# Attention trunk on one core: the V projection with the weights held still and a DMA transpose, one output store per pair and group, small operations in pairs

## The chip, the cores and the metric

The kernel runs on 1 core of one Trainium2 chip. The metric is the device time of one execution, in microseconds (us). Engines are named as in the profile: PE (TensorE matmul), PEld (its weight load), DVE (VectorE), ACT (ScalarE), POOL (GpSimd), SP (SyncE, here only a DMA queue).

## The reference, cut to what matters

One layer on x of 2048 tokens by 1024. The input projection gives q, k and v of 8 heads of banded attention (kind A) and of 4 pairs of heads of differential attention (kind B). What the change touches is the projection, both attentions and the way of their output into the output projection:

```python
h = rmsnorm(x, attn_norm_g[l])
proj = h @ w_in[l]
qa, ka, va, qb, kb, vb = jnp.split(proj, 6, axis=-1)
...
# kind A: 64-wide heads, 9 chunks of 64 keys behind and at the query's chunk
scores = jnp.where(valid, scores + bias[:, None], -jnp.inf)
p = jax.nn.softmax(scores, axis=-1).astype(v.dtype)
o = jnp.einsum("bhcqk,bckhd->bcqhd", p, vb)
...
# kind B: all earlier chunks, two maps per head
p = jax.nn.softmax(sc, axis=-1).reshape(b, B_HEADS, 2, Q_BLOCK, s)
w = p[:, :, 0] - lam * p[:, :, 1]
o = jnp.einsum("bhqk,bkhe->bqhe", w.astype(v.dtype), v)
...
x = x + jnp.concatenate([oa, ob], axis=-1) @ w_out[l]
```

Behind it stand a gated feed-forward part with a causal convolution and a last rmsnorm, which the change leaves alone.

## The kernel before

**Numbers.** Every matrix product is made of float16 halves: a value is split into a high and a low half (`split`: ACT writes the high one, DVE or POOL the low one), and a product is three matmuls per block of 128 rows (`TERMS`: high by high, high by low, low by high). With eight blocks of 128 in D a projection is 24 matmuls.

**Stages.** The attention part works pair of heads by pair of heads, in the order `ORDER = [4, 5, 0, 6, 1, 7, 2, 3]`: numbers from 4 up are kind B (`attn_b`), the others kind A (`attn_a`). A pair holds 128 columns of each of Q, K and V. Within a pair there are four groups of 512 tokens (`tg`), and in a group four tiles of 128 queries. The stages lie from about 100 to 1300 us: B 100 to 280, B 280 to 450, A 450 to 565, B 565 to 745, A 745 to 860, B 860 to 1040, then two A. After them come the output projection, whose first half fills the last stage, and the feed-forward part.

**One tile.** `scores` (L417, L419) makes 128 queries by up to 512 keys; DVE adds the bias and takes the running maximum (L466 in A, L516 in B); `nb` (L472, L520) turns the maximum into the exponent's bias, one operation per head; ACT takes the exponential (L473, L522) with its row sum. In B a tile wider than 1024 keys has two halves, whose row sums are added per head (L525); then the two maps are combined with `ratio` (L538 on DVE; for the second half of odd tiles L535 on ACT and L536 on POOL). The result is split into `phl` (ACT L474 or L540; low half on POOL L475 or L541, in A for one head on DVE), transposed by a DMA on SP into `pt` (L476, L543), multiplied with V (L487, L549) and scaled into `osb` (L489, L551).

**A group's end.** `store_oT` splits `osb` into `ohl` (L427 ACT, L428 DVE), transposes it on SP into `ost` (L432), and stores it with four DMAs on POOL (L437) into `oTd[NT, P, 2, NC-1, P]` in DRAM. The last pair's `ost_l` stays in SBUF. `out_proj` loads one tile of `oTd` at a time (L606), 3584 bytes per partition in one piece.

**Projections.** `project` (L365 to L374) holds the weights of Q or K still and streams 512 tokens: 24 matmuls 128x512. `proj_v` (L385 to L398) does it the other way round, since V is wanted with tokens on partitions: a tile of h is held still, the weights of 128 columns are streamed, 4 x 24 matmuls 128x128, and the sum is split straight into `vs`.

**What sets the order.** In the main loop a pair's stage first prepares the next pair's weights (`load_w`: DMA, squares on DVE, the scaling L331 and low half L333 on POOL, the high half L332 on ACT). Then for each group it writes Q of the next group, the group's four tiles at a raised priority, and K and V of the next pair for the same group. A scheduler makes each engine's order from priorities and its own times, so that the projections of the next pair fill PE between the tiles. Score rows are kept in "granules", one pool of 8 buffers: a B tile over 1024 keys takes four, the others two. There are four weight buffers `whl`, which the loads `oT` use later, and two `wraw`.

## Time and profile before

| What | Value |
|---|---|
| runs | 2644.75, 2649.1, 2653.84 us; median 2649.1 |
| the profiled execution | 2652.78 us, of it span 2651.0 us, mean granted clock of TensorE 0.95 |
| PE busy | 2405.8 us (91%) |
| DVE busy | 1949.0 us (74%) |
| ACT busy | 1402.0 us (53%) |
| POOL busy | 1246.5 us (47%) |

The shares are means over the attention, the output projection and the feed-forward part. The change touches the first two only, so the argument goes by stretches of time: the busy time of each engine in a stretch, and the rows of single instructions with their start and length. The granted clock is 1.00 at 2.4 GHz and 0.50 at 1.2 GHz; a mean between them is a mixture.

### The profile page before, as it was taken

To read this page: it belongs to the slowest core of one execution; us is meant where nothing else is said; L and a number is where in the kernel's file an instruction comes from. 1 tells how busy PE (TensorE), PEld (TensorE's weight loads), DVE (VectorE), ACT (ScalarE), POOL (GpSimd) and SP (SyncE) were. 2 spreads that over 40 slices of the span, in tenths; PEclk is the share of its full clock that TensorE was granted. 3 is DMA by queue.
4 is the path that set the end of the run, shared out by engine and by line. 5 is a ranking of instruction groups with operands and counts; after the bars stand their busy time and mean duration, and the time that the engine had idled before them with its cause. 6 is when DMAs were issued, how large, how long until landed. Compare 5 with 4: busy or idle time off the path is not lost.

```text
span 2651.0 us, 43815 instructions
## 1 busy us (share of the span) xinstructions
PE 2405.8 (91%) x15894; PEld 1245.1 (47%) x15894; DVE 1949.0 (74%) x4551; ACT 1402.0 (53%) x2431; POOL 1246.5 (47%) x1239
## 2 busy tenths in 40 slices
PE   5798897979788896899986999999999999999998
PEld 4554454545455454554432444444444444444443
DVE  6778798658976687676675688888887887656655
ACT  5456466545655466565543556666656564333332
POOL 2324345342542335222243466655566655756654
PEclk8899898989899897999988999999999999999999
DMA  7233445643465336778979533333333338432322
GB/s 205 55 60 75 85 83 109 113 99 60 85 120 111 73 68 151 147 175 199 282 231 218 139 105 124 109 100 124 111 113 121 100 102 320 174 107 86 126 91 76
DMA packets 571016, 333.42 MB, mean 126 GB/s; under 512 B 392024, under 2 KB 533648, under 8 KB 569392
## 3 DMA queue, kind: packets, MB, share of 16 engines
q1 hardware_dynamic: 551456, 301.46, 44.0%
q0 software_dynamic: 6752, 18.91, 2.4%
q10 hardware_dynamic: 12592, 10.26, 1.4%
q8 instruction: 124, 2.03, 0.3%
q14 instruction: 92, 0.75, 0.1%
HBM read 148.87 MB, written 85.21 MB: 88 GB/s over the span
## 4 chain that ended last, share of the span: by engine, by line
PE 37%; DVE 4%; POOL 3%; DMA 3%; issue 3%; ACT 2%; SPq 0%; DVEq 0%; ACTq 0%; POOLq 0%
PE mm L752 22%; PE mm L1151 13%; PE omm L616 2%; DMA wd<-gd 1%; DMA wdraw<-in_w_down_dram 1%; POOL wuhl L870 1%; ACT wuraw L852 1%; DVE Y L951 1%; DVE wdhl L782 1%; DVE hl L640 1%; DMA td<-hl 0%; ACT wdhl L779 0%; POOL wd L1128 0%; ACT Y L955 0%; SPq L986 0%
## 5 line engine op out<-in xcount | busy, mean ns | idle before, releaser
L752 PE MATMUL mm<-T,wuhl 128*128 128x512 f16 x3696 | 807.2, 381 | 28.1 <-ACT tmp L923 24.5
L752 PEld LDWEIGHTS <-wuhl 128*128 128x128 f16 x3696 | 362.7, 99 | 464.8 <-issue 34.5
L1151 PE MATMUL mm<-wd,ghl 128*128 128x512 f16 x1848 | 401.8, 380 | 3.4 <-ACT ghl L127 2.1
L372 PE MATMUL mm<-h,whl 128*128 128x512 f16 x1536 | 370.5, 390 | 0.0
L541 POOL TENSOR_TENSOR phl<-St,phl 128x1024 f16<-128x1024 f32 (+4 forms) x96 | 162.3, 1725 | 291.5 <-ACT phl L540 276.8
L417 PE MATMUL s<-ks,qs 128*128 128x128 f16 (+3 forms) x720 | 198.5, 298 | 101.5 <-DVE mx L466 47.2
L1151 PEld LDWEIGHTS <-ghl 128*128 128x128 f16 x1848 | 180.7, 98 | 223.8 <-ACT ghl L127 3.6
L951 DVE SCALAR_TENSOR_TENSOR Y<-U,taps,Y 128x1024 f32<-128x1024 f32 x176 | 256.6, 1458 | 4.0 <-ACT Y L947 2.4
L393 PE MATMUL mm<-whl,h 128*128 128x128 f16 x3072 | 236.6, 226 | 2.9 <-ACT h L127 2.9
L522 ACT ACTIVATE St<-St,nb,sc 128x1024 f32<-128x1024 f32 (+4 forms) x192 | 188.4, 982 | 85.1 <-DVE nb L520 80.9
L372 PEld LDWEIGHTS <-whl 128*128 128x128 f16 x1536 | 146.1, 101 | 173.8 <-issue 26.4
L127 ACT ACTIVATE ghl<-wd,gsc 128x384 f16<-128x384 f32 (+1 forms) x176 | 106.4, 659 | 197.1 <-DMA wd<-gd 90.2
L393 PEld LDWEIGHTS <-h 128*128 128x128 f16 x3072 | 186.8, 101 | 48.6 <-issue 24.4
L128 DVE SCALAR_TENSOR_TENSOR ghl<-wd,gsc,ghl 128x384 f16<-128x384 f32 (+1 forms) x176 | 137.5, 816 | 94.4 <-ACT ghl L127 93.7
L419 PE MATMUL s<-ks,qs 64*128 64x128 f16 (+3 forms) x720 | 187.3, 303 | 0.9 <-DVE qs L128 0.9
L475 POOL TENSOR_TENSOR phl<-St,phl 128x640 f16<-128x640 f32 (+2 forms) x64 | 84.4, 1339 | 219.6 <-ACT phl L474 195.9
L516 DVE CUSTOM_DVE_ANT_0 St<-s,near,mxb 128x512 f32<-128x512 f32 (+3 forms) x280 | 170.1, 624 | 23.5 <-PE s L419 18.9
L616 PE MATMUL omm<-wohl,oT 128*128 128x512 f16 x672 | 157.4, 387 | 13.9 <-DVE x L620 13.9
L861 POOL TENSOR_TENSOR Sx<-wuraw 128x512 f32<-128x512 f32 x44 | 78.0, 1775 | 168.8 <-ACT wuraw L852 159.8
L419 PEld LDWEIGHTS <-qs 64*128 64x128 f16 x720 | 57.6, 93 | 206.8 <-issue 186.1
L473 ACT ACTIVATE St<-St,nb,sc 128x640 f32<-128x640 f32 (+4 forms) x128 | 108.1, 845 | 77.0 <-DVE nb L472 76.0
L955 ACT ACTIVATE Y<-Y 128x1024 f32<-128x1024 f32 x44 | 46.5, 1057 | 183.8 <-DVE Y L951 183.8
(226 smaller groups left out, 4217.1 us busy)
## 6 DMA issues: line engine op xcount, KB each, us to landing
wd<-gd SPq DMA_DIRECT2D x88, 256.0 KB, 2.8
wuraw<-in_w_up_dram SPq DMA_DIRECT2D x42, 512.0 KB, 5.1
gd<-Y SPq DMA_DIRECT2D x42, 512.0 KB, 4.9
wdraw<-in_w_down_dram SPq DMA_DIRECT2D x154, 128.0 KB, 2.7
wd<-wdd SPq DMA_DIRECT2D x11, 1792.0 KB, 12.4
wdd<-wdhl SPq DMA_DIRECT2D x41, 448.0 KB, 2.6
wraw<-in_w_in_dram SPq DMA_DIRECT2D x24, 512.0 KB, 4.5
td<-hl SPq DMA_DIRECT2D x24, 512.0 KB, 3.9
```

The source lines that it names most:

```text
L128: V.scalar_tensor_tensor(lo, src, scale, hi, ALU.mult, ALU.subtract)
L372: nc.tensor.matmul(ps, lhsT=hl[:, a, c, :], rhs=h[:, b, c, :], start=n == 0, stop=n == 3 * NC - 1)
L393: nc.tensor.matmul(ps[:, t], lhsT=h[:, a, c, t * P:(t + 1) * P], rhs=hl[:, b, c, :], start=n == 0, stop=n == 3 * NC - 1)
L417: nc.tensor.matmul(ps[hd], lhsT=qs[:, hd, 0, qc], rhs=ks[:, hd, kc], start=True, stop=False)
L419: nc.tensor.matmul(ps[hd], lhsT=qs[a:b, hd, 1, qc], rhs=ks[a:b, hd, kc], start=False, stop=True)
L516: V.tensor_tensor_reduce(Sm[hd][g][:, a0:a0 + b - a], ps[hd][:, :b - a], bias, 1.0, m[hd], ALU.add, ALU.max, mx[:, hd, f:f + 1])
L522: A.activation(Sm[hd][g], Sm[hd][g], AF.Exp, bias=nb[:, hd:hd + 1], scale=w["sc"], accum_out=l[:, hd, g:g + 1])
L541: nc.gpsimd.tensor_tensor(hl[:, 1], Sm[0][g], hl[:, 0], ALU.subtract)
L616: nc.tensor.matmul(ps[n], lhsT=oc[:, a], rhs=wo[ORDER[c]][:, b, n * TG:(n + 1) * TG], start=k == 0, stop=k == 3 * NC - 1)
L752: nc.tensor.matmul(ps, lhsT=hl[:, a, wop, c * P:(c + 1) * P], rhs=Tt[:, b, c, :], start=start and k == 0, stop=k == 11, skip_group_check=n ...
L951: V.scalar_tensor_tensor(Y, self.U[j][:, tap:D + tap], self.u.taps[j][:, tap:tap + 1], Y, ALU.mult, ALU.add)
L1151: nc.tensor.matmul(ps[m].rearrange("p (c n) -> p c n", c=4), lhsT=g[kb][:, a, go], rhs=wd[kb][:, :, c_, wo_], start=kb == k0 and k == 0, s ...
```

## The change

1. V of every pair but the first is made by `project`, as Q and K are: 24 matmuls 128x512 with the weights held still. The result has V's columns on partitions. It is split into a granule `vt` and transposed by one DMA on SP into `vs`. The first pair keeps the old way.
2. `oTd` gets the shape `[NG, P, 2, NC-1, 4, P]`, and a pair and group is stored with one DMA on SP (pieces of 1 KB) rather than four on POOL. The load `oT` now gathers 14 pieces of 256 bytes per partition.
3. `nb` of both heads is one operation, and stands behind the maxima of both. The sum of the two halves' row sums in B is one operation for both heads.

```diff
--- before.py
+++ after.py
@@ -173,7 +173,7 @@
     cw = const.tile([P, 2 * NB, 3], F32, name="cw")
     cb = const.tile([P, 2 * NB], F32, name="cb")
     x1d = dram.tile([NT, P, D], F32, name="x1d")
-    oTd = dram.tile([NT, P, 2, NC - 1, P], F16, name="oTd")
+    oTd = dram.tile([NG, P, 2, NC - 1, 4, P], F16, name="oTd")
     rep = dram.tile([16, P, PROF], F32, name="rep")
     prof = dram.tile([16, PROF], F32, name="prof")
     td = dram.tile([2, 7, TG, 2, TG], F16, name="td")
@@ -383,18 +383,27 @@
             return ks
 
         def proj_v(w, tg):
+
+
             vs = kv.tile([P, 2, 4, P], F16, name="vs")
-            hl, h = w["hl"][2], hT[tg]
-            ps = ps_mm.tile([P, 4, P], F32, name="mm")
-            for t in range(4):
-                n = 0
-                for c in range(NC):
-                    for a, b in TERMS:
-                        nc.tensor.matmul(ps[:, t], lhsT=h[:, a, c, t * P:(t + 1) * P], rhs=hl[:, b, c, :],
-                                         start=n == 0, stop=n == 3 * NC - 1)
-                        n += 1
+            if "first" in w:
+                hl, h = w["hl"][2], hT[tg]
+                ps = ps_mm.tile([P, 4, P], F32, name="mm")
+                for t in range(4):
+                    n = 0
+                    for c in range(NC):
+                        for a, b in TERMS:
+                            nc.tensor.matmul(ps[:, t], lhsT=h[:, a, c, t * P:(t + 1) * P], rhs=hl[:, b, c, :],
+                                             start=n == 0, stop=n == 3 * NC - 1)
+                            n += 1
+                with tc.high_priority(offset=HP):
+                    split(vs[:, 0], vs[:, 1], ps, QS)
+                return vs
+            vt = granule("vt", TG, F16)
+            ps = project(w, tg, 2)
             with tc.high_priority(offset=HP):
-                split(vs[:, 0], vs[:, 1], ps, QS)
+                split(vt[:, 0], vt[:, 1], ps, QS)
+            nc.sync.dma_start_transpose(vs.rearrange("p a t q -> p (a t) q"), vt.rearrange("p a b -> p (a b)"))
             return vs
 
         def proj_q(w, tg):
@@ -433,8 +442,7 @@
             if last:
                 oTl[tg] = st
                 return
-            for t in range(4):
-                nc.gpsimd.dma_start(oTd[4 * tg + t, :, :, ORDER.index(c), :], st[:, :, t])
+            nc.sync.dma_start(oTd[tg, :, :, ORDER.index(c)], st)
 
         def pieces(k0, k1, cuts):
 
@@ -466,10 +474,10 @@
                         V.tensor_tensor_reduce(Sm[hd][:, a:b], ps[hd][:, :b - a], bias, 1.0, m[hd],
                                                ALU.add, ALU.max, mx[:, hd, part:part + 1])
                         m[hd] = mx[:, hd, part:part + 1]
+
+                V.tensor_scalar(nb, mx[:, :, 1 if F else 0], w["nsc"], LN14, ALU.mult, ALU.add)
                 for hd in range(2):
                     St = Sm[hd]
-
-                    V.tensor_scalar(nb[:, hd:hd + 1], m[hd], w["nsc"], LN14, ALU.mult, ALU.add)
                     A.activation(St, St, AF.Exp, bias=nb[:, hd:hd + 1], scale=w["sc"], accum_out=l[:, hd:hd + 1])
                     A.activation(hl[:, 0, hd], St, AF.Copy)
                     (nc.gpsimd if hd in AP else V).tensor_tensor(hl[:, 1, hd], St, hl[:, 0, hd], ALU.subtract)
@@ -516,13 +524,13 @@
                         V.tensor_tensor_reduce(Sm[hd][g][:, a0:a0 + b - a], ps[hd][:, :b - a], bias, 1.0, m[hd],
                                                ALU.add, ALU.max, mx[:, hd, f:f + 1])
                         m[hd] = mx[:, hd, f:f + 1]
+                V.tensor_scalar(nb, mx[:, :, f], w["nsc"], lnk, ALU.mult, ALU.add)
                 for hd in range(2):
-                    V.tensor_scalar(nb[:, hd:hd + 1], m[hd], w["nsc"], lnk, ALU.mult, ALU.add)
                     for g in range(len(gr)):
                         A.activation(Sm[hd][g], Sm[hd][g], AF.Exp, bias=nb[:, hd:hd + 1], scale=w["sc"],
                                      accum_out=l[:, hd, g:g + 1])
-                    if len(gr) == 2:
-                        V.tensor_tensor(l[:, hd, 0:1], l[:, hd, 0:1], l[:, hd, 1:2], ALU.add)
+                if len(gr) == 2:
+                    V.tensor_tensor(l[:, :, 0], l[:, :, 0], l[:, :, 1], ALU.add)
 
                 rl = tiny.tile([P, 2], F32, name="rl")
                 V.reciprocal(rl, l[:, :, 0])
@@ -603,7 +611,8 @@
                 for sd in range(2):
                     i = (2 * pc + sd) * 4 + t
                     oT = wpool.tile([P, 2, NC - 1, P], F16, name="oT", tag="whl", bufs=4)
-                    nc.sync.dma_start(oT, oTd[i])
+                    nc.sync.dma_start(oT.rearrange("p a c q -> p (a c) q"),
+                                      oTd[2 * pc + sd, :, :, :, t].rearrange("p a c q -> p (a c) q"))
                     lhs = [oT[:, :, c] for c in range(NC - 1)] + [oTl[2 * pc + sd][:, :, t]]
                     xt = kv.tile([P, D], F32, name="x1k", tag="qs", bufs=2) if pc and sd else \
                         wpool.tile([P, D], F32, name="x1", tag="wraw", bufs=2)
@@ -647,6 +656,7 @@
             return {"hl": {}, "E": {}}
 
         w = weights()
+        w["first"] = True
         groups, qn = {}, None
         xts, raws = [], []
         for k in FIRST:
```

The change moves instructions as well, since the scheduler makes its order anew. Two places follow, in the names of the programs; the number behind a name is the buffer.

POOL at the end of the first B stage. `phl` is the low half of a tile's result, `wraw` and `whl` the next pair's weights being scaled and split, `oTd` the store of the group before, and `St` from `St` the add of a tile's second half. Before, from the last half of tile 13 on:

```order
L541 TENSOR_TENSOR phl_3024<-St_2944,phl_3024 128x768
L331 TENSOR_TENSOR wraw_3445<-wraw_3445,ws_gs_3459 128x1024
L331 TENSOR_TENSOR wraw_3464<-wraw_3464,ws_gs_3478 128x1024
L437 DMA oTd_86<-ost_2659 256x1x128 x4
L541 TENSOR_TENSOR phl_3109<-St_3051,phl_3109 128x1024
L333 TENSOR_TENSOR whl_3447<-wraw_3445,whl_3447 128x1024
L541 TENSOR_TENSOR phl_3139<-St_3052,phl_3139 128x896
L333 TENSOR_TENSOR whl_3466<-wraw_3464,whl_3466 128x1024
L536 TENSOR_TENSOR St_3170<-St_3170,St_3172 128x1024
L541 TENSOR_TENSOR phl_3227<-St_3169,phl_3227 128x1024
```

After, from tile 12's splits on (L549 is the old L541, L544 the old L536):

```order
L333 TENSOR_TENSOR whl_3131<-wraw_3129,whl_3131 128x1024
L549 TENSOR_TENSOR phl_2652<-St_2596,phl_2652 128x1024
L333 TENSOR_TENSOR whl_3150<-wraw_3148,whl_3150 128x1024
L549 TENSOR_TENSOR phl_2682<-St_2597,phl_2682 128x640
L544 TENSOR_TENSOR St_2707<-St_2707,St_2709 128x768
L331 TENSOR_TENSOR wraw_3167<-wraw_3167,ws_gs_3181 128x1024
L549 TENSOR_TENSOR phl_2754<-St_2706,phl_2754 128x1024
L549 TENSOR_TENSOR phl_2785<-St_2707,phl_2785 128x768
L333 TENSOR_TENSOR whl_3169<-wraw_3167,whl_3169 128x1024
L549 TENSOR_TENSOR phl_2868<-St_2812,phl_2868 128x1024
L549 TENSOR_TENSOR phl_2898<-St_2813,phl_2898 128x896
L544 TENSOR_TENSOR St_2929<-St_2929,St_2931 128x1024
```

The store is gone. The weights stood among the splits of tiles 14 and 15 (`phl_3109`, `phl_3139`, `St_3170`); now they stand among those of tiles 12 and 13 (`phl_2652` to `phl_2785`), and the splits of tile 14 (`phl_2868`, `phl_2898`) and the add of tile 15 (`St_2929`) follow one another.

SP behind the second group's store of the first stage, before:

```order
L432 DMA_TRANSPOSE ost_2089<-ohl_2086 128x8x128
L543 DMA_TRANSPOSE pt_2494<-phl_2491 128x16x128
L543 DMA_TRANSPOSE pt_2524<-phl_2521 128x6x128
L543 DMA_TRANSPOSE pt_2592<-phl_2589 128x16x128
L543 DMA_TRANSPOSE pt_2623<-phl_2620 128x8x128
```

and after (L441 is the old L432, L551 the old L543):

```order
L441 DMA_TRANSPOSE ost_2008<-ohl_2005 128x8x128
L445 DMA oTd_86<-ost_2008 256x1x512
L406 DMA_TRANSPOSE vs_2530<-vt_2531 128x8x128
L551 DMA_TRANSPOSE pt_2334<-phl_2331 128x16x128
L551 DMA_TRANSPOSE pt_2364<-phl_2361 128x6x128
```

Between the transpose `ost` and the next tile's transpose `pt` now stand the store, which needs `ost` landed, and the transpose of a V block. Over the whole kernel the store stands straight behind its `ost` in 8 cases of 28, one row further in 18 and two in 2; behind the store comes a `pt` in 13 and a V transpose in 6, and behind a V transpose a `pt` in 22 of 28.

## Rows read from the trace of the kernel before

**Rows 1.** Busy time by stretch: us of PE, PEld, DVE, ACT, POOL; clock; DMA

```profile
100.00:1300.00 1200.00, 1042.95 (x9329) 606.39 (x9329) 906.19 (x2721) 683.11 (x1309) 449.10 (x344) 0.92 0.54 111
...
900.00:1000.00 100.00, 97.94 (x837) 54.72 (x835) 87.17 (x262) 63.48 (x123) 34.28 (x23) 1.00 0.39 70
```

**Rows 2.** The same view, the ends of the four B stages.

```profile
246.00:276.00 30.00, 8.85 (x62) 5.31 (x61) 29.09 (x62) 13.14 (x23) 19.35 (x12) 0.62 0.60 125
420.00:444.00 24.00, 11.58 (x67) 7.03 (x67) 21.11 (x52) 17.05 (x33) 20.56 (x13) 0.58 0.54 113
704.00:734.00 30.00, 10.75 (x65) 6.43 (x64) 28.71 (x61) 13.50 (x27) 19.71 (x12) 0.61 0.58 125
997.00:1027.00 30.00, 9.50 (x67) 5.71 (x67) 28.94 (x62) 13.51 (x25) 19.45 (x12) 0.68 0.61 126
```

**Rows 3.** Timeline of DVE: start, us, engine, line, op, out<-in, count.

```profile
262.86 11.32 DVE L538 SCALAR_TENSOR_TENSOR St<-St,ratio 128x1024 f32<-128x1024 f32 x1
...
428.71 8.81 DVE L538 SCALAR_TENSOR_TENSOR St<-St,ratio 128x1024 f32<-128x1024 f32 x1
...
721.20 11.33 DVE L538 SCALAR_TENSOR_TENSOR St<-St,ratio 128x1024 f32<-128x1024 f32 x1
...
1004.30 0.74 DVE L516 CUSTOM_DVE_ANT_0 St<-s,near,mxb 128x512 f32<-128x512 f32 x1
...
1013.94 11.32 DVE L538 SCALAR_TENSOR_TENSOR St<-St,ratio 128x1024 f32<-128x1024 f32 x1
```

**Rows 4.** Groups by form, whole run: busy us, mean ns, idle before.

```profile
L538 DVE SCALAR_TENSOR_TENSOR St<-St,ratio 128x1024 f32<-128x1024 f32 x36 | 93.2, 2588 | 0.5
```

**Rows 5.** Timeline of POOL at the end of the fourth B stage.

```profile
1010.92 2.83 POOL L437 DMA_DIRECT2D oTd<-ost  x4
1013.25 2.66 POOL L541 TENSOR_TENSOR phl<-St,phl 128x1024 f16<-128x1024 f32 x1
1015.35 2.63 POOL L333 TENSOR_TENSOR whl<-wraw,whl 128x1024 f16<-128x1024 f32 x1
...
1021.34 2.83 POOL L536 TENSOR_TENSOR St<-St 128x1024 f32<-128x1024 f32 x1
```

**Rows 6.** Timeline of PE there; in brackets the idle time before, its releaser.

```profile
1025.79 0.27 PE L417 MATMUL s<-ks,qs 128*128 128x128 f16 x1 [12.87 <-DVE mx L466]
```

**Rows 7.** Timeline of PE, unbroken runs of projection matmuls in other places.

```profile
954.70 3.30 PE L393 MATMUL mm<-whl,h 128*128 128x128 f16 x56
...
991.49 2.58 PE L393 MATMUL mm<-whl,h 128*128 128x128 f16 x43
...
1129.56 4.70 PE L372 MATMUL mm<-h,whl 128*128 128x512 f16 x21
...
1161.64 1.89 PE L372 MATMUL mm<-h,whl 128*128 128x512 f16 x8
```

**Rows 8.** Groups by line, whole run: busy us, mean ns, idle before.

```profile
L372 PE MATMUL mm<-h,whl 128*128 128x512 f16 x1536 | 370.5, 390 | 0.0
...
L393 PE MATMUL mm<-whl,h 128*128 128x128 f16 x3072 | 236.6, 226 | 2.9 <-ACT h L127 2.9
...
L520 DVE TENSOR_SCALAR nb<-mxb,nsc,lnk 128x1 f32<-128x1 f32 x128 | 32.4, 266 | 0.7
...
L525 DVE TENSOR_TENSOR lb<-lb 128x1 f32<-128x1 f32 x64 | 26.6, 416 | 10.3 <-ACT St L522 10.2
...
L472 DVE TENSOR_SCALAR nb<-mx,nsc 128x1 f32<-128x1 f32 x128 | 24.8, 205 | 0.8
```

**Rows 9.** Timeline of the SP queue: a transpose's issue.

```profile
1004.41 1.23 SPq L432 DMA_TRANSPOSE ost<-ohl  x1
```

**Rows 10.** DMA issues, whole run: count, KB each, median us to landing.

```profile
oTd<-ost POOLq DMA_DIRECT2D x112, 64.0 KB, 2.4
oT<-oTd SPq DMA_DIRECT2D x16, 448.0 KB, 4.8
...
ost<-ohl SPq DMA_TRANSPOSE x28, 3.2
```

## Prediction, made before the changed kernel ran

> **What bounds the kernel now.** I first read the busy table by stretch. Between 100 and 1300 us, where the eight attention stages run, PE is busy 1042.95 of 1200 us at a mean clock of 0.92; in the middle of a stage of kind B it is busy 97.94 of 100 us at clock 1.00, with DVE at 87.17 [rows 1]. So inside a stage PE is the bound and DVE is close behind: an instruction taken from DVE or POOL there is worth little, one taken from PE is worth nearly its own time. The 157 us that PE lacks lie in a few places. The same view at the ends of the four B stages shows PE busy 8.85, 11.58, 10.75 and 9.50 us in windows of 30, 24, 30 and 30 us, at a clock of 0.58 to 0.68, while DVE is busy nearly throughout [rows 2]: 114 - 40.7 = 73.3 us of idle PE in four places.
>
> I then read DVE's instructions there. In each window one instruction, the combine L538 of the stage's last tile, lasts 11.32, 8.81, 11.33 and 11.32 us [rows 3]. The 36 instructions of that shape take 93.2 us together [rows 4], so the other 32 take (93.2 - 42.8)/32 = 1.58 us. POOL's rows at the same times tell why: from 1010.92 on it runs without a gap, L437 (four stores), L541, L333, L541, L333, L536, and L538, begun at 1013.94, ends at 1025.26, when the POOL run has ended (1021.34 + 2.83 = 24.2) [rows 3, 5]. L538 reads two operands from SBUF, and stands still while POOL keeps SBUF busy. Behind it in DVE's order stand the first score operations of the next stage, and PE waits 12.87 us for one of them [rows 6]. It is this queue of weight preparation (L331, L333) and last tiles on POOL that sets the stage ends.
>
> **The change part by part.** The sum is made against the profiled run's own 2652.8 us; the median shown, 2649.1, is 3.7 lower, and I take that off at the end.
>
> *V by stationary weights*: 28 of 32 blocks change from 96 matmuls of 128 columns to 24 of 512. In runs at full clock 56 of the narrow ones end after 3.30 us and 43 after 2.58, so one more costs 0.72/13 = 0.055 us; 21 wide ones take 4.70 and 8 take 1.89, so one costs 2.81/13 = 0.216 [rows 7]. A block goes from 5.32 to 5.18: -0.14, and 28 blocks give -4. The runs are also cut up more rarely by other matmuls, for which I add 1: **-5** (bounds 0 and -45, rival B's). The Trainium skill, page "TensorE: Matmul & The Clock Gate", section Back-to-back issue gap, says that sustained streams need about 81 ns for 128 columns and 131 ns for 512. By that a block would go from 7.8 to 3.1 us, and 28 of them would give -130 us, an estimate from the page. The slopes above, 55 and 216 ns, contradict it in both terms, and the sum goes by them.
>
> *Paired small operations*: 128 operations L520 at 0.266 us and 128 L472 at 0.205 become half as many, and 64 L525 at 0.416 become 32 [rows 8]: 17 + 13 + 13 = 43 us less on DVE. In mid-stage PE covers them, so the bounds are 0 and -43; I take a fifth, since DVE's 87% against PE's 98% leaves little on the path: **-8**. The paired nb waits for both heads' maxima, so the exponential of head 0 starts later by up to one score operation (0.74 us for 512 columns [rows 3]); 128 tiles bound it by 95. ACT has slack and head 1 starts earlier: **+2**.
>
> *Stores leave POOL*: 28 times four issues of 2.83 us together [rows 5] are 79 us of POOL, and its wait for the transpose ahead of them goes. POOL is less than half busy (449 of 1200 [rows 1]), and only where it delays a tile's split does it count: **-3** (0 to -30).
>
> *Stage ends*: the program's order moves as well. The weight preparation stands some two tiles earlier on POOL, and the last tile's combine (now L546) has only splits and one add beside it there. On PE K and V of the last group come earlier in the new order, and Q of the next pair is the filler left for the last tiles. If the four combines fall from 42.8 us to 2.6 each (POOL still runs beside them, so above 1.58), 32 us go; the preparation now meets the combines of tiles 12 and 13, which have filler beside them, and I give 4 back: **-28**. Bounds: 0, and -88 if all of the idle 73 goes and the 40.7 busy us run at full clock rather than at about 0.62 (15 more).
>
> *SyncE*: the store waits in SP's order for the transpose ost, which lands 3.2 us after its issue [rows 10]; the issue itself occupies SP for 1.23 us [rows 9], and 28 transposes of V with the same price join. Queued behind are the transposes of the next probabilities (pt), for which PE's value matmuls wait. Each store then holds the queue by at most 3.2 + 1.23 less what stands between, and every V transpose by 1.23: 28 x 3.5 = 98 at most. Filler on PE covers most of it, and most stores fall where the next pt is not yet made: **+7**, a quarter of a us each (bounds 0 and 98).
>
> *The granule for V*: it takes one of eight score buffers for the time from split to landing, about the 3.2 us of the like transpose ost [rows 10]. That hurts only where a tile needs four buffers, 8 groups of tokens in the four B stages: 0 to 8 x 3.2 = 26, taken **+4**, since projection and tile run side by side only at times.
>
> *Reading the output back*: a load oT of 448 KB takes 4.8 us in pieces of 3584 bytes and will come in pieces of 256. The store oTd, 64 KB in such pieces, takes 2.4 [rows 10]; seven of them would be 16.8, so a load costs 0 to 12 more. Sixteen loads run ahead through four buffers, and only the first of each of two passes is exposed: 0 to 24, taken **+3**, because 2.4 us for a small transfer is mostly latency. The Trainium skill ("DMA: Bandwidth & Descriptors", Specifications) puts the least piece for full rate at 512 bytes, which speaks against this layout; at half rate two exposed loads would cost 2 x 4.8 = 10, an estimate, and the sum would be 7 higher.
>
> Sum: -5 - 8 + 2 - 3 - 28 + 7 + 4 + 3 = -28. 2652.8 - 28 - 3.7 = **2621**.
>
> **The rivals.** *C, the stall moves rather than goes.* POOL has the same weight work; packed at tiles 12 and 13 it can stop the combine there just as long, and the A stages may now end without filler. For it: the new order on POOL still has L333, split, L333, split, add, L331 in a row. Against it: these tiles have K and V matmuls beside them. Without the -28 the other terms give 0: 2649.
>
> *D, SyncE becomes the queue that delays* (the other side). If each store holds a pt transpose that is ready, at the last tile of a group or the first of the next, by x us more than I took, the cost is 28x. It eats the gain from x = 1.0, and the kernel is slower by over 0.3% from x = 1.3. Two thirds of the landing, x = 2.2, gives -28 + 62 = +34: 2683. For it: before, SP issued the transposes of pt with nothing waiting in front, whereas in the new order the store stands straight behind ost or one row later, and a pt behind it; and the first tiles of a group are short, so their pt is wanted early. Against: PE has Q, K and V matmuls to run while it waits.
>
> *B, V gains by the group means.* Over the whole run the narrow matmul takes 236.6/3072 = 0.077 us of PE and the wide one 370.5/1536 = 0.241 [rows 8], 7.4 against 5.8 a block: 28 x 1.6 = 45 instead of 5, so 2621 - 40 = 2581. The rule of the Trainium skill on the issue gap would point to this side, and further. Against: the first pair's blocks and the stretches at half clock are in that mean, and the first pair does not change.
>
> **How the numbers follow.** This forecast has 0.46, B 0.08, C 0.22, D 0.24. What a measurement of this kernel can tell from no change is about 0.3%, so faster is under 2641.2 and slower over 2657.0. The forecast's own range is 2596 to 2641; nearly all of it, B, and a little of C are faster: 0.46 + 0.08 + 0.04 = 0.58. The rest of C is within: 0.18. D is slower: 0.24. For 8 in 10 I leave out most of B below and the upper third of D with the worst of the forecast above: 2590 to 2680.
>
> **What would show it.** Right on the stage ends: no combine L546 of 8 us or more in the last tiles of B stages, and PE busy well over 12 us in those four windows. Right on V: wide matmuls with a slope of 0.216 and 112 x 6 = 672 more of them, total PE time nearly unchanged. Right on SyncE: PE's wait for pt grows by less than 10 us. C is right if L546 of tiles 12 and 13 lasts 6 us or more and PE idles beside it; D if SP waits long for ost with a finished split behind it and PE waits for pt by tens of us; B if PE's busy time falls by 40 us. The prediction as a whole is wrong if the idle time of PE from 100 to 1300 us doesn't fall.

## The result

The changed kernel takes 2565.5 us (median of 2562.97 to 2569.02), the kernel before 2646.9 in all runs taken beside it: a ratio of 0.9692 with a 95% interval of 0.9665 to 0.9720, 81 us less. The forecast was 2621 with a range from 2590 to 2680. The sign was right; the gain is three times what was summed and lies outside the range.

The profiled execution of after has a span of 2560.9 us (before 2651.0, so 90.1 less). The first line of its page, busy time and share of each engine:

```profile
PE 2389.8 (93%) x13878; PEld 1146.9 (45%) x13878; DVE 1894.7 (74%) x4391; ACT 1401.5 (55%) x2431; POOL 1171.0 (46%) x1127
```

PE was busy 2405.8 of 2651.0 us before. So PE's busy time fell by 16.0 and its idle time from 245.2 to 171.1, by 74.1. Where the idle time went is seen in the view of [rows 2], busy time by stretch. The four windows below lie as far from the ends of the B stages of after (the last `osb` of each) as those of before did from theirs (columns: stretch, length, busy us of PE, PEld, DVE, ACT, POOL, then granted clock, DMA share, GB/s):

```profile
246.00:276.00 30.00, 30.00 (x185) 14.27 (x186) 22.84 (x69) 20.61 (x39) 13.79 (x6) 0.89 0.64 121
427.00:451.00 24.00, 23.29 (x136) 11.71 (x137) 13.41 (x44) 15.02 (x29) 6.93 (x4) 0.80 0.47 92
674.00:704.00 30.00, 28.36 (x188) 14.39 (x188) 26.98 (x72) 16.00 (x31) 13.73 (x7) 0.86 0.69 135
945.00:975.00 30.00, 29.87 (x231) 16.09 (x229) 22.47 (x50) 21.27 (x41) 12.09 (x6) 0.99 0.76 159
```

PE is busy 111.5 of 114 us there, against 40.7. The idle 73.3 us have become 2.5. A second place had not been in the forecast: the first 30 us of a B stage that follows an A stage. Before (the fourth and the sixth stage):

```profile
560.00:590.00 30.00, 15.80 (x140) 10.56 (x139) 18.56 (x76) 12.92 (x29) 16.60 (x14) 0.71 0.36 84
854.00:884.00 30.00, 15.27 (x118) 9.62 (x117) 16.26 (x62) 12.15 (x26) 18.57 (x17) 0.66 0.38 91
```

and after:

```profile
545.00:575.00 30.00, 27.16 (x144) 12.81 (x145) 16.44 (x56) 11.24 (x26) 6.75 (x5) 0.87 0.39 95
805.00:835.00 30.00, 20.38 (x111) 10.10 (x112) 15.34 (x41) 10.66 (x24) 11.76 (x7) 0.77 0.47 101
```

28.9 idle us have become 12.5. The two places give 70.8 + 16.5 = 87 us; some 13 us of idle time have appeared elsewhere.

The combine that stood still 8.8 to 11.3 us at each B stage's end ([rows 3], 93.2 us for its 36 instructions in [rows 4]) is short now. The projections' groups of after follow it here, to be held against [rows 8] (groups of the whole run: busy us, mean ns, idle before):

```profile
L546 DVE SCALAR_TENSOR_TENSOR St<-St,ratio 128x1024 f32<-128x1024 f32 x36 | 58.1, 1615 | 0.7
...
L372 PE MATMUL mm<-h,whl 128*128 128x512 f16 x2208 | 535.1, 389 | 0.1
...
L396 PE MATMUL mm<-whl,h 128*128 128x128 f16 x384 | 29.7, 237 | 2.9 <-ACT h L127 2.9
```

What PE does in the two places is seen by the projection matmuls there. In the four end windows before has two of them, after 260 (70, 53, 63 and 74). The wide ones (L372) in the first of the four windows, before and after (stretch, length, busy us of PE and PEld with counts, clock, DMA share, GB/s); narrow ones (L393) stand in none of the four in before:

```profile
246.00:276.00 30.00, 0.00 (x0) 0.00 (x0) 0.62 0.60 125
```

```profile
246.00:276.00 30.00, 19.18 (x70) 7.13 (x71) 0.89 0.64 121
```

A projection block is 24 wide or 96 narrow matmuls. In before the eight stages hold 22.9, 11.5, 9.8, 14.7, 9.5, 14.3, 9.5 and 3.7 blocks; in after 25.5, 12.7, 6.8, 17.1, 6.9, 17.3, 9.7 and 0. In before the last tiles of a B stage have next to no projection beside them; the A stage then uses up 9.8 and 9.5 blocks, and the B stage behind it has 1.5 and 1.6 in its first 30 us. In after V, Q and K blocks run at the end of the B stage, the A stage has fewer, and 4.0 and 3.0 blocks stand in the first 30 us of the next B stage.

### The profile page after: what moved, and what is told of

The parts are those of the page before. It is cut to its first block, busy times and chain, and to the rows that moved or that the text cites. A ratio compares the mean times of both kernels' runs of the same rounds, so it can differ in the third digit from the quotient of the medians.

```text
span 2560.9 us, 39466 instructions
## 1 busy us (share of the span) xinstructions
PE 2389.8 (93%) x13878; PEld 1146.9 (45%) x13878; DVE 1894.7 (74%) x4391; ACT 1401.5 (55%) x2431; POOL 1171.0 (46%) x1127
## 4 chain that ended last, share of the span: by engine, by line
PE 53%; DMA 8%; DVE 8%; issue 4%; ACT 4%; POOL 2%; SPq 2%; ACTq 0%; DVEq 0%; POOLq 0%
PE mm L762 27%; PE mm L1161 13%; PE mm L372 7%; DMA pt<-phl 5%; PE omm L625 2%; PE s L428 2%; DMA wd<-gd 2%; PE s L426 1%; SPq L996 1%; PE o L557 1%; DVE St L524 1%; ACT St L481 1%; ACT phl L482 1%; DVE hl L649 1%; DVE St L546 1%
## 5 line engine op out<-in xcount | busy, mean ns | idle before, releaser
L372 PE MATMUL mm<-h,whl 128*128 128x512 f16 x2208 | 535.1, 389 | 0.1
L372 PEld LDWEIGHTS <-whl 128*128 128x128 f16 x2208 | 205.7, 100 | 250.1 <-issue 38.2
L549 POOL TENSOR_TENSOR phl<-St,phl 128x1024 f16<-128x1024 f32 (+4 forms) x96 | 155.7, 1632 | 304.2 <-ACT phl L548 292.6
L557 PE MATMUL o<-vs,pt 128*128 128x128 f16 x1632 | 123.9, 231 | 21.0 <-DMA pt<-phl 16.4
L792 DVE SCALAR_TENSOR_TENSOR wdhl<-wdraw,wd_sc,wdhl 128x128 f16<-128x128 f32 x132 | 134.6, 1038 | 11.6 <-ACT wdhl L789 10.9
```

The costliest lines, as they stand in the source:

```text
L372: nc.tensor.matmul(ps, lhsT=hl[:, a, c, :], rhs=h[:, b, c, :], start=n == 0, stop=n == 3 * NC - 1)
L549: nc.gpsimd.tensor_tensor(hl[:, 1], Sm[0][g], hl[:, 0], ALU.subtract)
L557: nc.tensor.matmul(o, lhsT=pt[:, a_, j], rhs=vs[:, c_, kt % 4, :], start=kt == 0 and k_ == 0, stop=kt == i and k_ == 2)
```

## The experiments

The first theory (O) was that the new order of the blocks, which comes with V, carries the gain; its rivals were that the stores do (S), or that the parts are needed together (P). Which of them fell is told at each run. All are compared with the kernel before on the same chip. PE busy and idle are of one execution, the profiled one; idle is its span less PE busy. For undo_v and o_after50 that execution took 2608.3 and 2649.7 us, so their busy and idle times add up to clearly more than the median.

| kernel | median us | ratio, 95% | PE busy | PE idle |
|---|---|---|---|---|
| before | 2646.9 | | 2405.8 | 245.2 |
| after | 2565.5 | 0.9692 [0.9665, 0.9720] | 2389.8 | 171.1 |
| v_only | 2578.1 | 0.9733 [0.9701, 0.9766] | 2394.3 | 181.8 |
| s_only | 2596.2 | 0.9805 [0.9773, 0.9838] | 2400.9 | 194.7 |
| n_only | 2626.5 | 0.9923 [0.9886, 0.9960] | 2406.3 | 218.9 |
| undo_v | 2596.3 | 0.9814 [0.9775, 0.9852] | 2411.0 | 195.5 |
| undo_s | 2575.3 | 0.9719 [0.9681, 0.9757] | 2394.0 | 180.1 |
| undo_n | 2584.0 | 0.9753 [0.9730, 0.9776] | 2397.3 | 186.1 |
| v_cut | 2591.7 | 0.9784 [0.9760, 0.9808] | 2383.3 | 201.0 |
| v_nodma | 2562.1 | 0.9681 [0.9657, 0.9706] | 2383.0 | 177.2 |
| s_pool1 | 2598.6 | 0.9821 [0.9804, 0.9839] | 2400.8 | 194.9 |
| s_sp4 | 2603.9 | 0.9838 [0.9821, 0.9855] | 2398.5 | 200.8 |
| all_v | 2589.9 | 0.9781 [0.9766, 0.9795] | 2392.2 | 192.1 |
| o_before | 2620.9 | 0.9889 [0.9858, 0.9921] | 2418.7 | 199.3 |
| o_sn | 2594.9 | 0.9796 [0.9768, 0.9824] | 2416.8 | 177.2 |
| o_after50 | 2640.9 | 0.9983 [0.9966, 0.9999] | 2456.0 | 191.9 |
| o_after100 | 2609.4 | 0.9848 [0.9813, 0.9883] | 2411.8 | 194.9 |
| nb_b | 2565.1 | 0.9689 [0.9668, 0.9709] | 2402.9 | 163.8 |
| a_pool1 | 2581.6 | 0.9755 [0.9727, 0.9784] | 2398.6 | 182.6 |

### Each part alone

**v_only**: part 1 of the change in the kernel before.

```diff
-            ps = ps_mm.tile([P, 4, P], F32, name="mm")
-            for t in range(4):
...
+            vt = granule("vt", TG, F16)
+            ps = project(w, tg, 2)
...
+            nc.sync.dma_start_transpose(vs.rearrange("p a t q -> p (a t) q"), vt.rearrange("p a b -> p (a b)"))
```

> The kernel before with the V part alone: stationary weights and the DMA transpose for all pairs but the first. Theory O (the moved order): in this kernel too the weight preparation of the next pair stands away from the last tiles of a B stage, so the long combine at the four stage ends goes and idle PE falls by 60 to 75 us in all; PE busy falls by 10 to 16; 2647 - 80 = 2560 to 2580. Rival S (stores): the gain hangs on POOL being free of the stores, and V alone gives no more than the forecast's V terms (-5 - 28 + 4): 2615 to 2625. Rival P (parts needed together): under half of the 81 us, 2607 or more.

70 us of the 81, as theory O said; rival P falls.

**s_only**: part 2 alone.

```diff
-            for t in range(4):
-                nc.gpsimd.dma_start(oTd[4 * tg + t, :, :, ORDER.index(c), :], st[:, :, t])
+            nc.sync.dma_start(oTd[tg, :, :, ORDER.index(c)], st)
```

> The kernel before with the store part alone: one DMA on SP per pair and group, and the loads in 256-byte pieces. Theory O: the weight preparation keeps its place among the last tiles of the B stages, the combine there still lasts 8 us or more, and the time stays within 8 us of 2647. Rival S: POOL without its waits for the transpose gives 30 us or more, 2615 or less. The forecast's own terms (-3 + 7 + 3) say 2654.

52 us, which theory O did not allow. Its order of the weight preparation on POOL is that of before, and yet no combine is held long there. Groups by form, s_only:

```profile
L537 DVE SCALAR_TENSOR_TENSOR St<-St,ratio 128x1024 f32<-128x1024 f32 x36 | 56.5, 1569 | 0.5
```

The ends of its B stages, in windows at the same distance from the end as in before:

```profile
231.00:261.00 30.00, 22.41 (x191) 13.71 (x190) 26.45 (x90) 19.61 (x36) 17.70 (x9) 0.77 0.40 81
408.00:432.00 24.00, 13.10 (x74) 7.21 (x74) 12.11 (x40) 13.31 (x23) 20.55 (x10) 0.56 0.62 129
668.00:698.00 30.00, 21.60 (x181) 14.24 (x180) 26.98 (x86) 20.74 (x38) 19.12 (x9) 0.67 0.51 104
954.00:984.00 30.00, 17.81 (x147) 11.48 (x146) 23.62 (x75) 19.46 (x37) 19.58 (x10) 0.74 0.51 108
```

PE is busy 74.9 of 114 us: the idle time there is 39.1, between the 73.3 of before and the 2.5 of after. With the long combines gone and POOL rid of its stores, some 34 us of idle PE have gone there; the other 37 go only where projections run at the stage ends.

**n_only**: part 3 alone.

```diff
-                    V.tensor_scalar(nb[:, hd:hd + 1], m[hd], w["nsc"], lnk, ALU.mult, ALU.add)
+                V.tensor_scalar(nb, mx[:, :, f], w["nsc"], lnk, ALU.mult, ALU.add)
...
-                    if len(gr) == 2:
-                        V.tensor_tensor(l[:, hd, 0:1], l[:, hd, 0:1], l[:, hd, 1:2], ALU.add)
+                if len(gr) == 2:
+                    V.tensor_tensor(l[:, :, 0], l[:, :, 0], l[:, :, 1], ALU.add)
```

> The kernel before with the paired small operations alone. Theory O: about 40 us of DVE time go, the long combines at the stage ends stay, and the time falls by 6 (the forecast's terms, -8 + 2) or up to 12: 2635 to 2641. Rival: DVE bounds the B stages, and 25 to 40 us go: 2607 to 2622.

About 20 us, between the two. Here too the 36 combines are short, though the four stores are still on POOL, at the first end in the order of before and at the fourth behind three more operations; theory O had expected the long ones to stay:

```profile
L538 DVE SCALAR_TENSOR_TENSOR St<-St,ratio 128x1024 f32<-128x1024 f32 x36 | 56.8, 1579 | 0.6
```

Yet its stage ends are far from filled (windows at the same distance from the ends):

```profile
243.00:273.00 30.00, 11.74 (x87) 5.98 (x86) 29.65 (x67) 17.99 (x32) 20.16 (x13) 0.75 0.56 110
417.00:441.00 24.00, 18.86 (x132) 12.95 (x132) 16.99 (x48) 17.00 (x33) 22.12 (x14) 0.62 0.62 137
690.00:720.00 30.00, 14.48 (x97) 8.87 (x95) 23.93 (x60) 19.56 (x34) 22.37 (x14) 0.64 0.53 113
979.00:1009.00 30.00, 14.68 (x94) 9.33 (x93) 21.28 (x55) 17.76 (x30) 21.76 (x13) 0.66 0.60 121
```

PE is busy 59.8 of 114 us: 54.2 us stay idle. So short combines alone are worth 19 us of idle PE there, and at most the 34 of s_only, where POOL's stores are gone as well.

### Each part taken back

**undo_v** (parts 2 and 3), **undo_s** (1 and 3), **undo_n** (1 and 2): the diffs above, read the other way, in after.

```diff
# undo_v
-        w["first"] = True
-            ps = project(w, tg, 2)
+            for t in range(4):
# undo_s
-            nc.sync.dma_start(oTd[tg, :, :, ORDER.index(c)], st)
+                nc.gpsimd.dma_start(oTd[4 * tg + t, :, :, ORDER.index(c), :], st[:, :, t])
# undo_n
-                V.tensor_scalar(nb, mx[:, :, f], w["nsc"], lnk, ALU.mult, ALU.add)
+                    V.tensor_scalar(nb[:, hd:hd + 1], m[hd], w["nsc"], lnk, ALU.mult, ALU.add)
```

> The kernel after with V made the old way in every pair, so stores and small operations alone. Theory O: the stage ends are as in the kernel before, 2630 to 2645. Rival S or the DVE rival: 2570 to 2615, most of the gain without V.

> The kernel after with the stores put back: four DMAs on POOL per pair and group, the old layout. Theory O2 (two kinds of idle place: B stages' ends, where POOL's backlog holds the combine, and B stages' starts, where no projection was left; V cures both, the stores alone cure the first): with V in, the stores add little, 2565 to 2580. Rival S (stores and V each take time of their own off the path): the stores' 52 us alone come back at least by half, 2590 or more.

> The kernel after with nb and the row sums of the halves per head again. Theory O2: DVE is covered by PE, 2560 to 2575. Rival (DVE bounds the B stages once the idle places are gone): the 43 us of DVE come back by a half, 2585 or more.

The eight combinations do not add up: V gives 70 us alone, 51 with the small operations in, 12 with the stores in and 31 with both. The stores give 52 alone, 10 on top of the other two; the small operations 21 alone, nothing beside the stores, 18 on top of the other two. The intervals behind the 12 and the 10 overlap. The parts share much of one loss, and the one that comes first takes most of it; the 18 and the 31 on top of the other two are not part of it. Rival S of these tests (stores take time of their own) falls with undo_s, undo_v's 2596 lies where its rivals had put it, against theory O, and undo_n's 2584 between its two expectations.

### What the store does

**s_pool1** (new layout, one store, POOL's queue) and **s_sp4** (old layout, four stores, SP's queue):

```diff
# s_pool1, against s_only
-            nc.sync.dma_start(oTd[tg, :, :, ORDER.index(c)], st)
+            nc.gpsimd.dma_start(oTd[tg, :, :, ORDER.index(c)], st)
# s_sp4, against before
-                nc.gpsimd.dma_start(oTd[4 * tg + t, :, :, ORDER.index(c), :], st[:, :, t])
+                nc.sync.dma_start(oTd[4 * tg + t, :, :, ORDER.index(c), :], st[:, :, t])
```

> The kernel before with the new layout and one store per pair and group, but on POOL's queue instead of SP's. Theory Q (POOL stands in its order behind the landing of ost, and runs its backlog as one train afterwards): the wait stays, so most of the 52 us of the stores alone is not had, 2625 to 2655. Rival L (four issues against one, or the layout): 2590 to 2605, as with the store on SP.

> The kernel before with the four old stores in the old layout on SP's queue instead of POOL's. Theory Q: POOL is free of the wait, 2590 to 2605 as with one store on SP. Rival L (the single store and its 1 KB pieces are what helps): 2625 or more. Rival D of the prediction (SP becomes the queue that delays, with four issues a store): over 2650.

Theory Q falls with the first: POOL waits for the transpose as long as before, and the time is 2599. The waits of s_pool1 and of before (us in total, times, longest):

```profile
POOL oTd L436 <- DMA ost<-ohl: 91.5, 17, 11.4
```

```profile
POOL oTd L437 <- DMA ost<-ohl: 92.7, 18, 9.3
```

Rival L in its second form (the single store and its larger pieces are what helps) falls with s_sp4, which keeps the four stores and the layout and takes 2604. In its first form (four issues against one) it stands for POOL's queue, with s_pool1's one store at 2599. What s_only, s_pool1 and s_sp4 have in common is that POOL no longer issues four stores in a row. The traces show what these four do. In before every long combine falls into a row of three or five POOL operations behind such stores, and in these rows each operation starts 0.5 to 0.6 us before the one ahead of it has ended (L541 at 1013.25 lasts 2.66 us, and L333 starts at 1015.35 [rows 5]). In the 14 kernels that don't issue four stores on POOL no two operations of the attention stages overlap by more than 0.16 us. A combine that meets a row there is held by one operation only. Timelines of DVE and POOL at the second stage end of s_only:

```profile
412.27 3.14 DVE L537 SCALAR_TENSOR_TENSOR St<-St,ratio 128x1024 f32<-128x1024 f32 x1
```

```profile
411.76 2.57 POOL L333 TENSOR_TENSOR whl<-wraw,whl 128x1024 f16<-128x1024 f32 x1
414.29 2.86 POOL L540 TENSOR_TENSOR phl<-St,phl 128x896 f16<-128x896 f32 x1
```

The combine ends at 415.41, 1.08 us behind L333 and in the middle of the operation that follows it without a gap. In none of the 18 other kernels does a combine last 4 us. n_only, v_only, undo_s and o_before keep the four stores and have such overlapping rows still, but at the stage ends no combine falls into one of them; which shift of their orders brought that about, the runs don't show.

### What the new V does

**v_cut**: the data flow of after, the matmuls of before.

```diff
-            ps = project(w, tg, 2)
+            for t in range(4):
+                n = 0
+                for c in range(NC):
+                    for a, b in TERMS:
+                        nc.tensor.matmul(ps[:, t * P:(t + 1) * P], lhsT=hl[:, a, c, :], rhs=h[:, b, c, t * P:(t + 1) * P],
```

> The kernel after with each V block of the 28 cut into four times 24 matmuls of 128 columns, weights still held and transposed as in after: the same data flow, the shape and number of matmuls of before. Theory O2 with the order as the means: the new order here holds 14.8 projection blocks in the two B stages that follow an A stage, as before does (14.5; after 17.0), but fewer in the A stages; half of V's further gain goes, 2575 to 2590. Rival W (wide matmuls are themselves cheaper on PE than the slopes said): 28 x 1.6 = 45 us come back, 2600 or more, with PE busy up by 30 us or more. Rival D (the data flow alone decides): 2560 to 2572.

26 us more than after, just above the range of theory O2 and below that of rival W, and PE is not busier but less busy:

```profile
PE 2383.3 (92%) x15894; PEld 1230.5 (48%) x15894; DVE 1895.8 (73%) x4391; ACT 1400.5 (54%) x2431; POOL 1176.6 (46%) x1127
```

Rival W falls: it asked for 30 us more PE time. All of the loss and more is idle time (201.0 against 171.1), and it lies where after has its blocks and v_cut has fewer; 19 us of it lie at the starts of its fourth and sixth stage:

```profile
537.00:567.00 30.00, 14.28 (x68) 6.70 (x69) 14.89 (x39) 11.11 (x23) 15.74 (x10) 0.64 0.39 96
819.00:849.00 30.00, 14.27 (x66) 6.56 (x65) 14.71 (x37) 11.36 (x25) 15.64 (x10) 0.62 0.40 96
```

and what PE waits for there (timeline; in brackets the idle time before and its releaser):

```profile
549.78 0.50 PE L565 MATMUL o<-vs,pt 128*128 128x128 f16 x3 [11.48 <-DMA pt<-phl]
```

**v_nodma**: the wide matmuls without transpose and granule. It leaves out the turn of V, so that V's columns stand where tokens should.

```diff
-            vt = granule("vt", TG, F16)
-            ps = project(w, tg, 2)
+            ps = project(w, tg, 2).rearrange("p (t q) -> p t q", t=4)
             with tc.high_priority(offset=HP):
-                split(vt[:, 0], vt[:, 1], ps, QS)
-            nc.sync.dma_start_transpose(vs.rearrange("p a t q -> p (a t) q"), vt.rearrange("p a b -> p (a b)"))
+                split(vs[:, 0], vs[:, 1], ps, QS)
```

> The kernel after without the V transposes and without their granule: the wide result is split straight into the buffer of V, whose columns then stand where tokens should (a part of the computation left out: the turn of V). It prices the transposes on SP and the granule. The forecast's terms (part of 7, and 4) say 5 to 10 us less than after, 2555 to 2560. Rival (the transposes are free beside the filler): 2562 to 2570. If the transposes' wait is what moved the order for the better: 2575 or more.

3 us less than after, with intervals that overlap: the 28 transposes on SP and the granule cost nothing that shows.

**all_v**: the first pair too.

```diff
-        w["first"] = True
```

> The kernel after with V of the first pair made the new way too. If what V gives is the place of the projection blocks in the later stages, the first pair adds nothing, 2560 to 2570. Rival: the start waits for four more transposes, 2570 to 2580. A gain over after of more than 8 us would say that the shape itself pays.

24 us more than after. Both expectations were too small. The loss is the start: in the first 100 us PE is busy 52.20 us, in after 67.97, and the first stage ends at 331 us where that of after ends at 301.

### The order alone

**o_before** and **o_sn**: one number, by how many places the scheduler raises a tile's instructions, in before and in undo_v. **o_after50** and **o_after100**: the same in after.

```diff
-HA = 1000
+HA = 50
```

> The kernel before with one number changed: the tiles of a group are raised by 50 places in the scheduler's order rather than by 1000, so that projections of the next pair go ahead of them more often. V, stores and small operations stay old. The order then holds 17 projection blocks in each of the two B stages that follow an A stage, as after does (before 14.5). Theory R (V's gain is the order of the blocks): idle PE at the starts and ends of the B stages falls from 122 to under 60 us, and the time is 2565 to 2590, v_only's 2578 give or take the 9 us that the wide matmuls save on PE. Rival W (V's own cost or data flow is what gained): 2620 or more.

> Stores and small operations as in after, V old, and the tiles raised by 50 instead of 1000. Theory R: with the order supplied, the missing V costs no more than its 9 us on PE, 2565 to 2585. Rival W: 2590 or more, as without the number (2596).

> The kernel after with the tiles raised by 50 instead of 1000: three more projection blocks go into the first stage, the others hold nearly as many as in after. Theory R: B starts and ends have their filler already, so no more than 10 us either way, 2555 to 2575.

> The same with 100: two more blocks in the first stage. Theory R: 2555 to 2575. If one of the two is under 2557, there is a version faster than both kernels.

In o_before the blocks per stage are 26.1, 12.4, 6.5, 17.2, 6.8, 17.2 and 9.8, as in after, and the starts are filled:

```profile
570.00:600.00 30.00, 29.01 (x221) 16.51 (x221) 18.32 (x65) 12.60 (x27) 9.16 (x8) 0.92 0.47 86
849.00:879.00 30.00, 28.62 (x218) 16.37 (x219) 17.31 (x63) 12.04 (x27) 9.34 (x9) 0.90 0.46 86
```

PE's idle time there is 2.4 us of 60, and at the four ends 9.1 of 114. So the order is the means by which both places fill. But it gives only 27 us: 45 us of idle time appear elsewhere, and PE is 13 us busier. Theory R as it stood, that the order is all that V brings, falls, and o_sn says the same; both times lie at the edge of what rival W had said. In o_sn, with stores and small operations in, the idle time comes to 177.2, near after's 171.1, yet it takes 29 us more, and 27.0 of the 33.1 us between the two spans are PE's busy time:

```profile
PE 2416.8 (93%) x15894; PEld 1244.0 (48%) x15894; DVE 1892.9 (73%) x4391; ACT 1399.8 (54%) x2431; POOL 1176.9 (45%) x1127
```

Between o_before and v_only, which also differ by V with blocks in like places, it is 24.4 us of busy time. So in these two pairs, whose blocks stand alike, the kernel with the new V has about 25 us less of busy time. That V is the cause is not shown. Both pairs differ in the scheduler's number as well; at the same number, 50, the kernel with the new V is the busier one (o_after50 2456.0, o_sn 2416.8); and nb_b is 13 us busier than after with the same matmuls. The width of the matmuls alone doesn't do it, since v_cut has the narrow ones and the lowest busy time but one. Which operand is held still, how finely the blocks are cut up between the tiles' matmuls, and the clock that each order gets were not told apart.

After with 50 or 100 is worse by 75 and 44 us, against every expectation. More of the same order does not pay.

### The small operations in B, and the store on POOL in after

**nb_b**: one column per operation again, in the new place.

```diff
-                V.tensor_scalar(nb, mx[:, :, f], w["nsc"], lnk, ALU.mult, ALU.add)
+                for hd in range(2):
+                    V.tensor_scalar(nb[:, hd:hd + 1], mx[:, hd, f:f + 1], w["nsc"], lnk, ALU.mult, ALU.add)
```

> The kernel after with nb of B as two operations of one column, still behind both heads' maxima. In after the 64 paired ones take 35.1 us, no less than the 128 single ones of before (32.4), because some last up to 1.97 us while POOL runs. Theory H (the two-column form is held by POOL, the one-column form is not): none of the 128 lasts over 0.3 us, about 33 us in all; the end moves little by it. Rival: it was chance, and single ones are held as well. The order holds 15.4 and 16.0 projection blocks in the B stages behind A stages (after 17.0 and 16.7): 2560 to 2585.

Theory H holds. Single instructions of this line in before, after and nb_b (duration in ns: least, median, most):

```profile
L520 DVE TENSOR_SCALAR nb<-mxb,nsc,lnk x128: 253/267/275, 97.0 to 1009.1; 128x1 f32<-128x1 f32 x128
```

```profile
L527 DVE TENSOR_SCALAR nb<-mxb,nsc,lnk x64: 271/288/1967, 97.0 to 960.6; 128x2 f32<-128x2 f32 x64
```

```profile
L528 DVE TENSOR_SCALAR nb<-mxb,nsc,lnk x128: 249/265/276, 96.3 to 960.1; 128x1 f32<-128x1 f32 x128
```

The longest of after, and POOL beside it (timelines of DVE and POOL):

```profile
654.05 1.97 DVE L527 TENSOR_SCALAR nb<-mxb,nsc,lnk 128x2 f32<-128x2 f32 x1
```

```profile
653.86 3.24 POOL L549 TENSOR_TENSOR phl<-St,phl 128x1024 f16<-128x1024 f32 x2 [2.30 <-ACT phl L548]
```

At the end it makes no difference: 2565.1 against 2565.5.

**a_pool1**: after with its store on POOL.

```diff
-            nc.sync.dma_start(oTd[tg, :, :, ORDER.index(c)], st)
+            nc.gpsimd.dma_start(oTd[tg, :, :, ORDER.index(c)], st)
```

> The kernel after with its one store per pair and group on POOL's queue instead of SP's. If SP's wait for ost costs after anything, this is faster, 2550 to 2560; if POOL's does, slower, 2570 to 2585; if neither counts, 2560 to 2570.

16 us more. In the changed kernel the store belongs on SP. No version was faster than after by more than the measurement can tell.

## Why the prediction was wrong

**The bound and the place: right.** PE was the bound, its idle time lay at the ends of the B stages, and the change removed it there. The sign followed.

**Stage ends, -28: mis-sized, and this is the step that failed.** It held two things and priced one. The long combines were priced at 32 less 4. Where they go and no projections come, idle PE there falls by 19 (n_only) to 34 us (s_only), so that price was sound. The second thing was said in the same paragraph, that Q of the next pair "is the filler left for the last tiles", but it was read as what remains and not as what is added: the four windows, with two projection matmuls in before, hold 260 in after, and PE's idle time there falls by 70.8, not 28. The term had a lower bound of -88, worked out from just this idle time. The range did not keep it: it was built from the chances of the cases and stopped at 2590, where the bounds should have taken it to 2621 - 60 = 2561.

**The starts of B stages: missed.** The idle 28.9 us there stood in the trace of before and entered no term. An order that moves blocks out of the A stages fills them: 16.5 us of it in after, 26.6 in o_before, where the order is all that changed.

**The price of V on PE, -5: low.** PE's busy time fell by 16.0, of which 4.7 lie behind the attention stages, where both kernels run the same 5979 matmuls and no projection block stands. The slope of the wide matmul in after is the one used (two of its unbroken runs):

```profile
554.15 5.13 PE L372 MATMUL mm<-h,whl 128*128 128x512 f16 x23
...
559.45 2.11 PE L372 MATMUL mm<-h,whl 128*128 128x512 f16 x9
```

(5.13 - 2.11)/14 = 0.216 us. So the slopes are right for an unbroken run; what the broken ones cost, the forecast had put at 1, and no run here prices it. Rival B said 45 us by the groups' busy time, and that time did fall as it said, from 607.1 us (L372 and L393) to 564.8, by 42.3. But a group's busy time counts the stretches in which matmuls of two groups overlap for both: all groups of PE add up to 2609.5 us in before, where PE is busy 2405.8, and to 2564.1 in after, where it is busy 2389.8. PE's own time fell by 16. Rival B came nearest the measured time with 2581, by the wrong mechanism. By the page named with it, "TensorE: Matmul & The Clock Gate" of the Trainium skill, section Back-to-back issue gap, the saving would be 130 us, an estimate; the busy times of the runs differ by 16 to 27.

**The costs of the V path and the store, +14: not there.** SP's store waits 23.0 us in all for its transpose, and PE waits no longer for pt than before. Waits in after (us in total, times, longest):

```profile
SPq L445 <- DMA ost<-ohl: 23.0, 14, 3.3
...
PE o L557 <- DMA pt<-phl: 16.4, 5, 8.1
```

and in before:

```profile
PE o L549 <- DMA pt<-phl: 16.6, 6, 5.3
```

So rival D, the slower side, was wrong: filler covers the queue. The V transposes and the granule cost nothing (v_nodma), and a load of oT in pieces of 256 bytes lands 5.0 us after its issue instead of 4.8:

```profile
oT<-oTd SPq DMA_DIRECT2D x16, 448.0 KB, 5.0
```

The rule of the Trainium skill on pieces under 512 bytes ("DMA: Bandwidth & Descriptors", Specifications) has no price here that the landing shows.

**Small operations, -8 and +2: the sum within what was measured, its working wrong.** They were to take 43 us from DVE. The groups of after, beside [rows 8]:

```profile
L527 DVE TENSOR_SCALAR nb<-mxb,nsc,lnk 128x2 f32<-128x2 f32 x64 | 35.1, 549 | 0.5
...
L478 DVE TENSOR_SCALAR nb<-mx,nsc 128x2 f32<-128x2 f32 x64 | 17.4, 272 | 0.6
...
L533 DVE TENSOR_TENSOR lb<-lb 128x2 f32<-128x2 f32 x32 | 8.8, 275 | 7.8 <-ACT St L530 7.8
```

83.8 us have become 61.3, and none of the gain is in B's nb: 35.1 for 32.4. Most of it is in the sum of the halves, whose 0.416 us in before was a mean of work and waiting (below). On the end the part is worth between nothing and 21 us, depending on what else is in.

**Stores, -3: low where it came first.** They were priced as time of POOL; what they did was to make the rows of overlapping POOL operations that held the combines, and the prediction's "POOL keeps SBUF busy" didn't see them as the reason. Alone the change of the stores gives 52 us (idle PE falls by 50.5, of which 34 at the stage ends), and on top of the other parts 10.

**Rival C** (the stall moves) did not happen: 36 combines take 58.1 us, and PE at the starts and ends is busy.

## What to carry to other kernels

Where PE is the bound and idles in a few places, list all of them with their length, and ask of a new order which work stands in each; a change that lets independent matmuls reach those places can be worth more than any instruction that it saves. Where several edits each dissolve the same stall, price the stall once and expect the edits not to add up; and let the bound of the largest term set the edge of the range.

## What the runs showed of the hardware

A DVE instruction with two SBUF inputs that meets a running POOL operation stands still until that operation ends; behind POOL's own four stores it can stand still until a whole row has ended. In s_only the combine begins 0.51 us into L333 and ends 1.08 us behind it, beside the next operation; so it is with all 209 combines of the 19 traces that met two POOL operations one close behind the other. In before it is held over the rest of one and four more, 11.32 us, in a row whose operations overlap [rows 3, 5]. Of the six combines that met such a row, four in before and two in v_only, five lasted past its second operation. Why the operations overlap behind the stores, the runs don't show. The Trainium skill ("SBUF — State Buffer", Who interferes with whom) says that such an instruction and one of GpSimd that reads SBUF exclude each other for the length of an instruction; s_only agrees, and the rows behind the stores of before show a hold over five.

A `tensor_scalar` of one column is not held by POOL, one of two columns is: at most 276 ns in 128 instructions of nb_b, 37 of which began while a POOL operation ran, and 275 in before; up to 1967 ns in 64 of after. The same section of the Trainium skill counts tensor_scalar among the operations that can take the shared ports; that two columns do and one does not is what these runs add. With two inputs in SBUF one column is held too, the sum of the halves in before:

```profile
L525 DVE TENSOR_TENSOR lb<-lb x64: 146/155/3379, 174.9 to 1012.7; 128x1 f32<-128x1 f32 x64
```

The same matmuls can cost PE more by their order: o_after50 has the matmuls of after, 21 us more idle time and 66 us more busy time, at a lower mean clock. Its span and mean granted clock, and those of after:

```profile
core 0: 2647.9 us, clock 0.939
```

```profile
core 0: 2560.9 us, clock 0.956
```

Why its order draws the lower clock was not tried.
